# Sums of weight quarters for a seven-part product, made by adding transfers instead of by GpSimd and VectorE

## The chip, the cores and the metric

One Trainium2 chip; the kernel runs on 1 of its cores. The metric is the time of one execution on the device, in microseconds. The core's engines work side by side: TensorE (PE) does matrix products into PSUM, VectorE (DVE), ScalarE (ACT) and GpSimd (POOL) do elementwise work, SyncE (SP) issues most transfers, which 16 DMA engines carry out. GpSimd and ScalarE can issue transfers too. Each engine runs its own queue in order and waits for others by semaphores.

## What is computed

A decoder trunk of four layers on x of 512 tokens by 1024 features in float32. Each layer is a mixer and a dense SwiGLU feed-forward network (FFN), both behind an RMS norm and added to the residual stream:

```python
for i in range(DEPTH):                       # DEPTH = 4
    kind, j = i % 3, i // 3
    h = rmsnorm(x, norm_mix_g[i])
    if kind == 0:   m = short_conv_mixer(h, conv_w_in[j], conv_w[j], conv_w_out[j])
    elif kind == 1: m = chunked_sgu_mixer(h, ...)
    else:           m = retention_mixer(h, ret_w_in[j], ret_w_out[j])
    x = x + m
    h = rmsnorm(x, norm_ffn_g[i])
    x = x + (silu(h @ w_gate[i]) * (h @ w_up[i])) @ w_down[i]   # 1024 -> 2816 -> 1024
return rmsnorm(x, final_norm_g)
```

The products that the change concerns are h @ w_gate, h @ w_up (four FFNs) and h @ conv_w_in (the mixers of layers 0 and 3).

## The kernel before

Features lie on the 128 partitions, tokens along the free dimension. Weights are streamed from HBM in the order of use. The list `chunks` holds that order, and `weights()` prepares up to `AHEAD = 4` chunks ahead, but no further than the first seven-part chunk behind the present one. Every operand is split into two float32r parts, a high one (cast on ScalarE, line 157) and a low one (subtraction on VectorE, line 158), and each product is three matmuls: high by high, high by low, low by high.

The products named above go by Winograd's form of Strassen's method. A chunk is two blocks of 128 output features. Its weights are loaded in two halves of the input features, each half a tile "raw" of 128 x 1024 numbers, 512 KB, which holds four quarters a11, a12, a22 and a21 of 128 KB. `prepare7` makes four sums of quarters in a tile "sums" of the same size: s1, s2 and s4 on GpSimd (lines 131 to 133, each on the result of the one before), s3 on VectorE (line 134). Then three quarters of raw and the four sums are split. `columns7` makes seven products of 12 matmuls of 256 columns each from them, with the right operands xs (quarters of the normed input) and xt (sums of its quarters, from `operand_sums`), and adds up the results in PSUM and with copies in SBUF. The last of the seven parts and what follows (`late`, `held`) are issued while the next chunk is under way. The first chunk of such a layer (in layer 0 the first three) goes by four plain products (`columns4`), which need no sums.

In an FFN the chunks of gate and up alternate; a part of two or three pairs is followed, after the next gate chunk, by `leave`: the down product of the part's hidden features, in 8 blocks of output features of 12 or 18 matmuls of 512 columns.

The pools decide how far loads run ahead: "raw" has 4 buffers, "sums" has 2 (one chunk), the split parts of raw quarters ("w7") and of sums ("wp") have 4 each of high and low. The order of instructions on each engine is set by a scheduler at build time. The rows below write "q" behind an engine for its issuing queue.

Of the kernel before, what the change touches and what calls it, by code (L numbers as in the profile page):

```python
# [17 lines left out]
P = 128  # L18
# [3 lines left out]
NB = D // P            # feature blocks of the residual stream  # L22
NT = T // P            # token blocks
FF = 2816
NF = FF // P
H = T // 2             # tokens of half the sequence
FF_PARTS = ((0, 2), (2, 5), (5, 8), (8, 11))  # pairs of hidden blocks, by part of an FFN
# [8 lines left out]
LAG = 3                # blocks of u that are ahead of the mixing of v  # L36
SOON = 100             # instructions that urgent ones may pass in the scheduler's order
BEGUN = 4              # blocks whose products begin before the last of their operands are ready
AHEAD = 4              # weight chunks prepared ahead of their matmuls


class Kernel:
# [19 lines left out]
    def dense(self):  # L62
        """Memory of the layers whose products take seven parts."""
# [10 lines left out]
    @contextmanager  # L74
    def mixed(self):
        """Memory of the other layers."""
        with self.tc.tile_pool(name="blk", bufs=29, reuse_waits="tile") as self.blk:
            yield

# [17 lines left out]
    def plan7(self, src, plain=False):  # L97
        """Two blocks of columns, for columns4 if plain, else for columns7."""
        self.chunks.append((src, 0, plain))
# [14 lines left out]
    def prepare7(self, i):  # L114
        """Two blocks of columns, as the seven left operands of Winograd's form of Strassen's product."""
# [3 lines left out]
        for half in range(2):  # L119
            raw = self.raw.tile([P, NB // 4, 4, P], F32, tag="raw", name=f"raw{i}{half}")  # L120
            nc.sync.dma_start(raw, src[half])
            if plain:
                h, l = (self.wp.tile([P, NB // 4, 4, P], F32R, tag=part, name=f"w{part}{i}{half}") for part in "hl")
                self.split(raw, h, l)
                for j in range(4):
                    out[j] += [(h[:, k, j], l[:, k, j]) for k in range(NB // 4)]
                continue
            sums = self.sums.tile([P, NB // 4, 4, P], F32, tag="sums", name=f"sums{i}{half}")
            a11, a12, a22, a21 = (raw[:, :, j] for j in range(4))
            s1, s2, s3, s4 = (sums[:, :, j] for j in range(4))  # L130
            nc.gpsimd.tensor_add(s1, a21, a22)  # L131
            nc.gpsimd.tensor_sub(s2, s1, a11)  # L132
            nc.gpsimd.tensor_sub(s4, a12, s2)  # L133
            nc.vector.tensor_sub(s3, a11, a21)  # L134
            for x, n, first, pool in ((raw, 3, 0, self.w7), (sums, 4, 3, self.wp)):
                h, l = (pool.tile([P, NB // 4, n, P], F32R, tag=part, name=f"w{part}{i}{half}{n}") for part in "hl")
                self.split(x[:, :, :n], h, l)
                for j in range(n):
                    out[first + j] += [(h[:, k, j], l[:, k, j]) for k in range(NB // 4)]
# [15 lines left out]
    def split(self, src, h, l):  # L155
        """A float32 tile as two float32r tiles whose sum it is."""
# [9 lines left out]
    def product(self, ps, terms, first=True, last=True, more=False):  # L166
        """ps (+)= sum of lhsT.T @ rhs over (lhs_h, lhs_l, rhs_h, rhs_l), the last term's at the end;
        more: added to a finished sum."""
# [12 lines left out]
    def columns(self, name, acts):  # L181
        """One block of output features (on partitions), for all tokens."""
# [14 lines left out]
    def begin(self, name, acts):  # L197
        """The start of columns(), with the weights of the rest."""
# [5 lines left out]
    def columns7(self, name, then, hold=False):  # L204
        """Two blocks of output features of the residual stream. then() gets them as [P, 2 * T], when the
        next product is under way."""
# [29 lines left out]
        part(c5, 6, xs, 2, False)  # L236
        add(y[:, :H], c5, u2)
        part(c1, 5, xt, 2, False)
        add(y[:, 2 * H : 3 * H], c1, m5)

        def end():
            part(c1, 2, xt, 3, False)
            nc.scalar.copy(y[:, 3 * H :], c1)
# [4 lines left out]
    def columns4(self, name, then, hold=False):  # L248
        """The same by four products of blocks, for which the sums of the operand needn't be ready."""
# [16 lines left out]
    def finish(self, hold=False):  # L266
        """The rest of the last columns7, and what is done with its outcome (and those before it) unless on hold."""
# [8 lines left out]
    def rows(self, name, acts):  # L276
        """512 output features for each block of tokens (on partitions)."""
# [17 lines left out]
    def squares(self, src, add=None):  # L295
        """Running sum, over feature blocks, of the squares."""
# [12 lines left out]
    def rsqrt(self, ps, out, t):  # L309
        """out = ps ** -0.5, with a Newton step."""  # L310
# [7 lines left out]
    def scale_of(self, mean, r, t, *sums):  # L318
        """Each token's 1 / rms, on all partitions."""
# [8 lines left out]
    def diagonal(self, eye):  # L328
        """The matrix that mean_d is the inverse of, on vectors: D on the diagonal."""
# [8 lines left out]
    def scale_of_tokens(self, total):  # L338
        """Each token's 1 / rms, with tokens on partitions: a column for 128 of them."""
# [12 lines left out]
    def spread(self, r, t):  # L352
        """The same on all partitions, in PSUM."""
# [7 lines left out]
    def scale_in_psum(self):  # L361
        """Each token's 1 / rms, on all partitions."""
        return self.spread(self.scale_of_tokens(self.sum), self.hid.tile([P, 2 * T], F32, tag="hid", name="rs")[:, :T])

# [1 line left out]
    def operand(self, m, g):  # L366
        """x's block m as a part of the next product's operand."""
# [592 lines left out]
```

## Time and profile before

| | us |
|---|---|
| median of 2 runs | 2485.22 (2484.79 to 2485.66) |
| span of the profiled execution | 2484.2 |
| TensorE busy in it | 2417.6 (97%) |
| VectorE busy | 1836.7 (74%) |
| ScalarE busy | 1132.3 (46%) |
| GpSimd busy | 890.0 (36%) |

The profile is of one execution, and its span is the time from the first to the last instruction; the median of the runs lies 1.0 us above it. Busy times of engines overlap and don't add up. A group row gives the line of the code, the engine, the operation, the tile written and the tiles read, the shapes and the count, then the busy time in us and the mean of one in ns, and behind the second bar the idle time of the engine just before.

### The profile page before, as it was taken

How to read it: one execution, taken by the hardware profiler on the slowest of the kernel's cores; microseconds unless marked ns; L12 is line 12 of the kernel's file. 1: busy time of each engine (PE TensorE's matmuls, PEld its weight loads, DVE VectorE, ACT ScalarE, POOL GpSimd, SP SyncE). 2: the span in 40 equal slices, each digit the busy share in tenths (PEclk: the TensorE clock that was granted, in tenths of full speed). 3: DMA queues.
4: the chain of work that ended last, by engine and by line, in shares of the span. 5: the costliest groups of instructions: out<-in, count | busy, mean ns of one | idle time of the engine just before them, and what ended most of it. 6: DMA issues, size and time to landing. Idle time of an engine off the chain costs nothing.

```text
span 2484.2 us, 37622 instructions
## 1 busy us (share of the span) xinstructions
PE 2417.6 (97%) x14892; PEld 2179.7 (88%) x14892; DVE 1836.7 (74%) x2236; ACT 1132.3 (46%) x1638; POOL 890.0 (36%) x788
## 2 busy tenths in 40 slices
PE   7999999999999999999999999999999899999998
PEld 6988989988888899998888888799999788889988
DVE  7988878763757887767565465988767898978776
ACT  6455445443324544534333334545435545545443
POOL 5536533520101643442000000834433744733530
PEclk9999999999999999999999999999999999999999
DMA  4141333334332233233223131233234124133231
GB/s 154 62 145 53 116 111 95 97 115 119 94 103 92 68 111 122 88 97 122 95 72 94 60 123 58 91 107 115 85 98 132 52 69 153 52 119 103 85 112 59
DMA packets 78832, 242.09 MB, mean 97 GB/s; under 512 B 8768, under 2 KB 12864, under 8 KB 78656
## 3 DMA queue, kind: packets, MB, share of 16 engines
q1 hardware_dynamic: 77568, 238.65, 30.3%
q8 instruction: 116, 1.90, 0.3%
q10 hardware_dynamic: 1088, 1.05, 0.1%
q14 instruction: 60, 0.49, 0.1%
HBM read 237.56 MB, written 2.10 MB: 96 GB/s over the span
## 4 chain that ended last, share of the span: by engine, by line
PE 75%; DVE 16%; issue 5%; ACT 2%; POOL 1%; DMA 0%; SPq 0%; DVEq 0%; ACTq 0%; POOLq 0%
PE out L177 26%; PE pu L177 16%; PE pg L177 15%; PE pv L177 7%; DVE wl L158 6%; PE pc L177 2%; PE q L177 2%; PE k L177 2%; PE pb L177 2%; DVE sums L134 2%; DVE puy L512 1%; PE pz L177 1%; DVE xl L375 1%; PE po L177 1%; DVE pgy L488 1%
## 5 line engine op out<-in xcount | busy, mean ns | idle before, releaser
L157 ACT CAST wh<-raw 128x768 fp32r<-128x768 f32 (+3 forms) x500 | 425.1, 858 | 572.5 <-PE out L177 193.5
L158 DVE TENSOR_TENSOR wl<-raw,wh 128x768 fp32r<-128x768 f32 (+3 forms) x500 | 557.6, 1134 | 136.7 <-ACT wh L157 136.3
L131 POOL TENSOR_TENSOR sums<-raw 128x256 f32<-128x256 f32 x208 | 243.3, 1170 | 795.8 <-DMA raw<-in_ffn_w_up 360.7
L157 ACT CAST wh<-sums 128x1024 fp32r<-128x1024 f32 x208 | 212.2, 1046 | 182.6 <-POOL sums L133 78.0
L177 PE MATMUL out<-hidl,wh 128*128 128x512 f32 (+1 forms) x736 | 278.3, 380 | 0.0
L158 DVE TENSOR_TENSOR wl<-sums,wh 128x1024 fp32r<-128x1024 f32 x208 | 260.9, 1279 | 22.1 <-ACT wh L157 18.8
L177 PE MATMUL out<-hidh,wh 128*128 128x512 f32 (+1 forms) x736 | 274.6, 381 | 0.0
L133 POOL TENSOR_TENSOR sums<-raw,sums 128x256 f32<-128x256 f32 x208 | 230.1, 1107 | 10.4
L132 POOL TENSOR_TENSOR sums<-sums,raw 128x256 f32<-128x256 f32 x208 | 217.9, 1048 | 10.6
L177 PE MATMUL pg<-xl,wh 128*128 128x256 f32 (+1 forms) x672 | 201.9, 316 | 9.6 <-DVE xl L375 9.6
L422 DVE TENSOR_TENSOR x<-out,x 128x512 f32<-128x512 f32 x192 | 130.2, 683 | 107.0 <-PE out L177 105.9
L177 PE MATMUL out<-hidh,wl 128*128 128x512 f32 (+1 forms) x736 | 205.4, 380 | 0.0
L177 PE MATMUL pg<-xh,wh 128*128 128x256 f32 (+1 forms) x672 | 200.9, 315 | 0.0
L177 PE MATMUL pu<-tl,wh 128*128 128x256 f32 x704 | 185.4, 284 | 5.1 <-DVE tl L158 5.1
L177 PE MATMUL pu<-xl,wh 128*128 128x256 f32 (+1 forms) x656 | 190.0, 306 | 0.0
L177 PE MATMUL pu<-xh,wh 128*128 128x256 f32 (+1 forms) x656 | 189.7, 306 | 0.0
L134 DVE TENSOR_TENSOR sums<-raw 128x256 f32<-128x256 f32 x208 | 153.3, 752 | 44.1 <-DMA raw<-in_ffn_w_up 37.9
L177 PE MATMUL pu<-th,wh 128*128 128x256 f32 x704 | 185.5, 285 | 0.0
L177 PE MATMUL pg<-th,wh 128*128 128x256 f32 x640 | 168.3, 284 | 6.9 <-DVE pgy L224 6.9
L177 PE MATMUL pg<-tl,wh 128*128 128x256 f32 x640 | 167.3, 283 | 0.0
L177 PEld LDWEIGHTS out<-hidl,wh 128*128 128x128 f32 x736 | 138.6, 188 | 25.1
L177 PEld LDWEIGHTS out<-hidh,wh 128*128 128x128 f32 x736 | 137.8, 188 | 25.0
(261 smaller groups left out, 6064.5 us busy)
## 6 DMA issues: line engine op xcount, KB each, us to landing
raw<-in_ffn_w_gate SPq DMA_DIRECT2D x88, 512.0 KB, 3.6
raw<-in_ffn_w_up SPq DMA_DIRECT2D x88, 512.0 KB, 3.6
raw<-in_ffn_w_down SPq DMA_DIRECT2D x96, 384.0 KB, 3.3
raw<-in_conv_w_in SPq DMA_DIRECT2D x48, 512.0 KB, 3.7
raw<-in_sgu_w_v SPq DMA_DIRECT2D x16, 512.0 KB, 3.6
raw<-in_sgu_w_u SPq DMA_DIRECT2D x16, 512.0 KB, 3.5
raw<-in_sgu_w_out SPq DMA_DIRECT2D x16, 512.0 KB, 3.5
raw<-in_ret_w_qk SPq DMA_DIRECT2D x16, 512.0 KB, 3.6
```

The source lines that it names most:

```text
L131: nc.gpsimd.tensor_add(s1, a21, a22)
L132: nc.gpsimd.tensor_sub(s2, s1, a11)
L133: nc.gpsimd.tensor_sub(s4, a12, s2)
L134: nc.vector.tensor_sub(s3, a11, a21)
L157: self.nc.scalar.copy(h, src)
L158: self.nc.vector.tensor_sub(l, src, h.bitcast(F32))
L177: nc.tensor.matmul(ps, x, y, start=first and i == 0, stop=last and i == len(seq) - 1, skip_group_check=more)
L375: nc.vector.scalar_tensor_tensor(l[:, s], x[:, s], gm, h[:, s].bitcast(F32), ALU.mult, ALU.subtract)
L422: nc.vector.tensor_add(x[:, s], ps, x[:, s])
L488: self.nc.vector.tensor_mul(y, y, r.unsqueeze(1).broadcast_to([P, 2, T]))
L512: nc.vector.tensor_mul(y[:, s], y[:, s], g[:, s])
```

## The change

Three of a half's quarters are still loaded into raw (384 KB). The tile of sums is filled by transfers alone: SyncE loads the last quarter into all four places (a load that reads it four times), and three transfers issued by GpSimd add other quarters on top of what lies there: the third quarter to places 1 to 3, the first to places 2 to 4, the second to place 3. Each adds to bytes that the one before has written. The quarters and the sums get another sign and order for this, so that each sum is one of plus signs; the signs are made good where the products are added up (`columns7`: two slots exchanged, one add becomes a multiply by -1 and a subtraction, one copy a multiply by -1) and in the sums of the right operand (`operand_sums`: all four on VectorE, where two had been on GpSimd). The weights are laid out on the host so that a quarter is 1 KB in a row on each partition. Comments and docstrings went too.

```diff
 def prepare7(self, i):
-            raw = self.raw.tile([P, NB // 4, 4, P], F32, tag="raw", name=f"raw{i}{half}")
-            nc.sync.dma_start(raw, src[half])
...
-            sums = self.sums.tile([P, NB // 4, 4, P], F32, tag="sums", name=f"sums{i}{half}")
-            a11, a12, a22, a21 = (raw[:, :, j] for j in range(4))
-            s1, s2, s3, s4 = (sums[:, :, j] for j in range(4))
-            nc.gpsimd.tensor_add(s1, a21, a22)
-            nc.gpsimd.tensor_sub(s2, s1, a11)
-            nc.gpsimd.tensor_sub(s4, a12, s2)
-            nc.vector.tensor_sub(s3, a11, a21)
+            raw = self.raw.tile([P, 3, NB // 4, P], F32, tag="raw", name=f"raw{i}{half}")
+            sums = self.sums.tile([P, 4, NB // 4, P], F32, tag="sums", name=f"sums{i}{half}")
+            block = lambda j, n=1: src[half][:, j : j + 1].broadcast_to([P, n, NB // 4, P])
+            nc.sync.dma_start(raw, src[half][:, :3])
+            nc.sync.dma_start(sums, block(3, 4))
+            nc.gpsimd.dma_start(sums[:, :3], block(2, 3), accum_op=ALU.add)
+            nc.gpsimd.dma_start(sums[:, 1:], block(0, 3), accum_op=ALU.add)
+            nc.gpsimd.dma_start(sums[:, 2:3], block(1), accum_op=ALU.add)
             for x, n, first, pool in ((raw, 3, 0, self.w7), (sums, 4, 3, self.wp)):
-                self.split(x[:, :, :n], h, l)
+                self.split(x, h, l)
 def columns7(self, name, then, hold=False):
-        part(c5, 6, xs, 2, False)
+        part(c5, 5, xs, 2, False)
         add(y[:, :H], c5, u2)
-        part(c1, 5, xt, 2, False)
-        add(y[:, 2 * H : 3 * H], c1, m5)
+        part(c1, 6, xt, 2, False)
+        with self.tc.high_priority(SOON):
+            nc.vector.scalar_tensor_tensor(y[:, 2 * H : 3 * H], c1, -1.0, m5, ALU.mult, ALU.subtract)
...
-            nc.scalar.copy(y[:, 3 * H :], c1)
+            nc.scalar.mul(y[:, 3 * H :], c1, -1.0)
 def operand_sums(self, k, g):
-        nc.vector.tensor_sub(t1, b12, b11)
-        nc.gpsimd.tensor_sub(t2, b22, t1)
+        nc.vector.tensor_sub(t1, b11, b12)
         nc.vector.tensor_sub(t3, b22, b12)
-        nc.gpsimd.tensor_sub(t4, b21, t2)
+        nc.vector.scalar_tensor_tensor(t2, t1, -1.0, b22, ALU.mult, ALU.subtract)
+        nc.vector.scalar_tensor_tensor(t4, t2, -1.0, b21, ALU.mult, ALU.subtract)
```

How it moves instructions, at one place in the first FFN, where the chunk of an up product follows that of a gate product. On GpSimd before, the sums of the two halves of a gate chunk (its tiles are sums_3094 and sums_3109 before, sums_3093 and sums_3108 now; the number behind a tile is its place in the program; a row names line, operation, tile written, tiles read, shape and the semaphores waited for):

```order
L131 TENSOR_TENSOR sums_3094<-raw_3092 128x2x128 [waits DMAHW6_49,DVE_49]
L132 TENSOR_TENSOR sums_3094<-sums_3094,raw_3092 128x2x128 [waits Pool_49]
L131 TENSOR_TENSOR sums_3109<-raw_3107 128x2x128 [waits DMAHW7_49,DVE_49]
L133 TENSOR_TENSOR sums_3094<-raw_3092,sums_3094 128x2x128 [waits Pool_49]
L132 TENSOR_TENSOR sums_3109<-sums_3109,raw_3107 128x2x128 [waits Pool_49]
L133 TENSOR_TENSOR sums_3109<-raw_3107,sums_3109 128x2x128 [waits Pool_49]
```

GpSimd now, for the same chunk and for the one before it; "DMAHW" is the landing of a load by SyncE, "DMASW" that of a transfer issued by GpSimd:

```order
L134 DMA sums_2960<-in_ffn_w_up 128x3x256 [waits DMAHW6_49,DMASW0_49,DVE_49]
L134 DMA sums_2975<-in_ffn_w_up 128x3x256 [waits DMAHW7_49,DMASW1_49,DVE_49]
L135 DMA sums_2960<-in_ffn_w_up 128x3x256 [waits DMASW2_49]
L135 DMA sums_2975<-in_ffn_w_up 128x3x256 [waits DMASW3_49]
L136 DMA sums_2960<-in_ffn_w_up 128x256 [waits DMASW4_49]
L136 DMA sums_2975<-in_ffn_w_up 128x256 [waits DMASW5_49]
L134 DMA sums_3093<-in_ffn_w_gate 128x3x256 [waits DMAHW2_49,DMASW6_49,DVE_49]
L134 DMA sums_3108<-in_ffn_w_gate 128x3x256 [waits DMAHW3_49,DMASW7_49,DVE_49]
L135 DMA sums_3093<-in_ffn_w_gate 128x3x256 [waits DMASW0_49]
L135 DMA sums_3108<-in_ffn_w_gate 128x3x256 [waits DMASW1_49]
L136 DMA sums_3093<-in_ffn_w_gate 128x256 [waits DMASW2_49]
L136 DMA sums_3108<-in_ffn_w_gate 128x256 [waits DMASW3_49]
```

Three operations on data for each half have become three transfers for each half, taken in turn for the two halves; each waits for the landing of the one before it on the same half, and the first also for the load by SyncE and for VectorE's last use of the buffer.

On SyncE before, the loads of three chunks (two halves each) around the same place:

```order
L121 DMA raw_2959<-in_ffn_w_up 128x1024 [waits DMAHW0_49,DVE_49,Pool_49]
L121 DMA raw_2974<-in_ffn_w_up 128x1024 [waits DMAHW1_49,DVE_49,Pool_49]
L121 DMA raw_3092<-in_ffn_w_gate 128x1024 [waits DMAHW2_49,DVE_49,Pool_49]
L121 DMA raw_3107<-in_ffn_w_gate 128x1024 [waits DMAHW3_49,DVE_49,Pool_49]
L121 DMA raw_3223<-in_ffn_w_up 128x1024 [waits DMAHW4_49,DVE_49,Pool_49]
L121 DMA raw_3238<-in_ffn_w_up 128x1024 [waits DMAHW5_49,DVE_49,Pool_49]
```

SyncE now:

```order
L132 DMA raw_2959<-in_ffn_w_up 128x768 [waits DMAHW4_49,DVE_49]
L132 DMA raw_2974<-in_ffn_w_up 128x768 [waits DMAHW5_49,DVE_49]
L132 DMA raw_3092<-in_ffn_w_gate 128x768 [waits DMAHW6_49,DVE_49]
L132 DMA raw_3107<-in_ffn_w_gate 128x768 [waits DMAHW0_49,DVE_49]
L133 DMA sums_2960<-in_ffn_w_up 128x4x256 [waits DMASW6_49,DMASW4_49,DMAHW7_49,DMASW0_49,DVE_49]
L133 DMA sums_2975<-in_ffn_w_up 128x4x256 [waits DMASW7_49,DMASW5_49,DMAHW1_49,DMASW1_49,DVE_49]
L132 DMA raw_3223<-in_ffn_w_up 128x768 [waits DMAHW2_49,DVE_49]
L132 DMA raw_3238<-in_ffn_w_up 128x768 [waits DMAHW3_49,DVE_49]
L133 DMA sums_3093<-in_ffn_w_gate 128x4x256 [waits DMASW6_49,DMASW4_49,DMAHW6_49,DMASW2_49,DVE_49]
L133 DMA sums_3108<-in_ffn_w_gate 128x4x256 [waits DMASW7_49,DMASW5_49,DMAHW7_49,DMASW3_49,DVE_49]
```

Each half has two loads in place of one. The load into the sums of a chunk (sums_3093) stands behind the raw loads of the chunk after it (raw_3223), and waits for VectorE's subtraction from the same buffer's former sums.

On ScalarE now, the casts of the sums of the same chunk and what stands around them:

```order
L229 COPY pgm<-pg_3253 128x256 [waits PE_49]
L159 CAST wh_3230<-raw_3223 128x768 [waits DMAHW0_49,PE_49]
L159 CAST wh_3245<-raw_3238 128x768 [waits DMAHW1_49,PE_49]
L246 ACTIVATE puy<-pu_3122 128x256 [waits PE_49]
L159 CAST hidh<-puy 128x1024 [waits DVE_49]
L159 CAST wh_3103<-sums_3093 128x1024 [waits DMASW4_49,DMAHW2_49,DMASW2_49,DMASW0_49]
L159 CAST wh_3118<-sums_3108 128x1024 [waits DMASW5_49,DMAHW3_49,DMASW3_49,DMASW1_49]
L231 COPY pgm<-pg_3254 128x256 [waits PE_49]
L235 COPY pgm<-pg_3253 128x256 [waits PE_49]
```

The same place of ScalarE before:

```order
L157 CAST wh_2981<-raw_2974 128x768 [waits DMAHW5_49,PE_49]
L243 COPY puy<-pu_2874 128x256 [waits PE_49]
L157 CAST hidh<-puy 128x1024 [waits DVE_49]
L157 CAST wh_3103<-sums_3094 128x1024 [waits PE_49,Pool_49]
L157 CAST wh_3118<-sums_3109 128x1024 [waits PE_49,Pool_49]
L227 COPY pum<-pu_3122 128x256 [waits PE_49]
L229 COPY pum<-pu_3123 128x256 [waits DVE_49,PE_49]
L157 CAST wh_3099<-raw_3092 128x768 [waits DMAHW6_49,PE_49]
L157 CAST wh_3114<-raw_3107 128x768 [waits DMAHW7_49,PE_49]
L243 COPY pgy<-pg_2989 128x256 [waits PE_49]
```

The casts stand where they stood, behind the end of the chunk before and ahead of the copies of the next part's results (pgm, line 231 now); what they wait for is no longer GpSimd but the landings of four transfers.

## Rows read from the trace of the kernel before

**Rows 1.** The page: span, and busy time of each engine.
```profile
span 2484.2 us, 37622 instructions
...
PE 2417.6 (97%) x14892; PEld 2179.7 (88%) x14892; DVE 1836.7 (74%) x2236; ACT 1132.3 (46%) x1638; POOL 890.0 (36%) x788
```

**Rows 2.** The chain that ended last: start us, us, what; one part, and a down product.
```profile
286.13 2.88 PE pg L177 x24
289.01 1.45 PE pu L177 x12
...
344.38 25.87 PE out L177 x114
```

**Rows 3.** Timeline of SyncE's queue, dense stretch: start us, us, engine, line, operation, count.
```profile
292.10 1.74 SPq L121 DMA_DIRECT2D raw<-in_ffn_w_up  x2
302.98 1.74 SPq L121 DMA_DIRECT2D raw<-in_ffn_w_gate  x2
313.64 19.78 SPq L108 DMA_DIRECT2D raw<-in_ffn_w_down  x8
```

**Rows 4.** Busy time by window, two chunks of the dense stretch; columns in the first row.
```profile
core 0: us, PE busy (x) PEld busy (x) DVE busy (x) ACT busy (x) POOL busy (x), PEclk, DMA share, GB/s
292.10:313.64 21.54, 21.54 (x182) 21.54 (x181) 20.96 (x23) 11.39 (x18) 14.67 (x13) 1.00 0.31 99
```

**Rows 5.** Waits (us in total, times, longest), and GpSimd's timeline for one chunk.
```profile
POOL sums L131 <- DVE wl L158: 355.3, 107, 11.0
...
298.69 1.65 POOL L131 TENSOR_TENSOR sums<-raw 128x256 f32<-128x256 f32 x1 [2.95 <-DVE wl L158]
300.42 0.80 POOL L132 TENSOR_TENSOR sums<-sums,raw 128x256 f32<-128x256 f32 x1
...
305.00 0.74 POOL L133 TENSOR_TENSOR sums<-raw,sums 128x256 f32<-128x256 f32 x1
```

**Rows 6.** Instructions on tile "sums", 290 to 330 us: ns min/median/max, first and last start.
```profile
L157 ACT CAST wh<-sums x6: 1028/1044/1050, 296.1 to 318.6; 128x1024 fp32r<-128x1024 f32 x6
L158 DVE TENSOR_TENSOR wl<-sums,wh x6: 1214/1218/1220, 297.4 to 320.4; 128x1024 fp32r<-128x1024 f32 x6
```

**Rows 7.** Groups of instructions: what | busy us, mean ns | idle before, releaser.
```profile
L131 POOL TENSOR_TENSOR sums<-raw 128x256 f32<-128x256 f32 x208 | 243.3, 1170 | 795.8 <-DMA raw<-in_ffn_w_up 360.7
...
L132 POOL TENSOR_TENSOR sums<-sums,raw 128x256 f32<-128x256 f32 x208 | 217.9, 1048 | 10.6
...
L133 POOL TENSOR_TENSOR sums<-raw,sums 128x256 f32<-128x256 f32 x208 | 230.1, 1107 | 10.4
...
L134 DVE TENSOR_TENSOR sums<-raw 128x256 f32<-128x256 f32 x208 | 153.3, 752 | 44.1 <-DMA raw<-in_ffn_w_up 37.9
```

**Rows 8.** VectorE's timeline, dense stretch: sums by VectorE, and adds from PSUM.
```profile
299.66 1.84 DVE L134 TENSOR_TENSOR sums<-raw 128x256 f32<-128x256 f32 x2
...
307.72 0.42 DVE L224 TENSOR_TENSOR puy<-pu,pum 128x256 f32<-128x256 f32 x1
```

**Rows 9.** DMA: queue (packets, MB, share of engines); issues with KB each, us to landing.
```profile
q1 hardware_dynamic: 77568, 238.65, 30.3%
...
raw<-in_ffn_w_gate SPq DMA_DIRECT2D x88, 512.0 KB, 3.6
...
raw<-in_ffn_w_down SPq DMA_DIRECT2D x96, 384.0 KB, 3.3
...
raw<-in_conv_w_out SPq DMA_DIRECT2D x16, 128.0 KB, 2.1
```

More of the change, by code (lines that the diff above doesn't have):

```diff
@@ L119, in prepare7 @@
         for half in range(2):
-            raw = self.raw.tile([P, NB // 4, 4, P], F32, tag="raw", name=f"raw{i}{half}")
-            nc.sync.dma_start(raw, src[half])
             if plain:
-                h, l = (self.wp.tile([P, NB // 4, 4, P], F32R, tag=part, name=f"w{part}{i}{half}") for part in "hl")
+                raw = self.raw.tile([P, 4, NB // 4, P], F32, tag="raw", name=f"raw{i}{half}")
+                nc.sync.dma_start(raw, src[half])
+                h, l = (self.wp.tile([P, 4, NB // 4, P], F32R, tag=part, name=f"w{part}{i}{half}") for part in "hl")
@@ L124, in prepare7 @@
                 self.split(raw, h, l)
                 for j in range(4):
-                    out[j] += [(h[:, k, j], l[:, k, j]) for k in range(NB // 4)]
+                    out[j] += [(h[:, j, k], l[:, j, k]) for k in range(NB // 4)]
                 continue
-            sums = self.sums.tile([P, NB // 4, 4, P], F32, tag="sums", name=f"sums{i}{half}")
-            a11, a12, a22, a21 = (raw[:, :, j] for j in range(4))
-            s1, s2, s3, s4 = (sums[:, :, j] for j in range(4))
-            nc.gpsimd.tensor_add(s1, a21, a22)
@@ L135, in prepare7 @@
+            nc.gpsimd.dma_start(sums[:, :3], block(2, 3), accum_op=ALU.add)
+            nc.gpsimd.dma_start(sums[:, 1:], block(0, 3), accum_op=ALU.add)
+            nc.gpsimd.dma_start(sums[:, 2:3], block(1), accum_op=ALU.add)
             for x, n, first, pool in ((raw, 3, 0, self.w7), (sums, 4, 3, self.wp)):
-                h, l = (pool.tile([P, NB // 4, n, P], F32R, tag=part, name=f"w{part}{i}{half}{n}") for part in "hl")
-                self.split(x[:, :, :n], h, l)
+                h, l = (pool.tile([P, n, NB // 4, P], F32R, tag=part, name=f"w{part}{i}{half}{n}") for part in "hl")
+                self.split(x, h, l)
@@ L138, in prepare7 @@
                 for j in range(n):
-                    out[first + j] += [(h[:, k, j], l[:, k, j]) for k in range(NB // 4)]
+                    out[first + j] += [(h[:, j, k], l[:, j, k]) for k in range(NB // 4)]
         return out
@@ L880, in columns_by_two @@
     n, k, m = w.shape
-    w = w.reshape(n, 2, k // (4 * P), 2, P, m // (2 * P), 2, P).transpose(0, 5, 1, 4, 2, 6, 3, 7)
-    return np.ascontiguousarray(w.reshape(n, m // (2 * P), 2, P, k // (4 * P), 4, P)[..., [0, 1, 3, 2], :])
+    w = w.reshape(n, 2, k // (4 * P), 2, P, m // (2 * P), 2, P).transpose(0, 5, 1, 4, 6, 3, 2, 7)
+    return np.ascontiguousarray(w.reshape(n, m // (2 * P), 2, P, 4, k // (4 * P), P)[:, :, :, :, [0, 1, 3, 2]])
 def columns_first(w, parts=1):
```

## The prediction

> **What bounds the kernel now.** I read the busy shares first, then one dense stretch, then who releases the buffers of the sums. TensorE is busy for 2417.6 of 2484.2 us [rows 1], so all its idle time is 67 us, and no change to the other engines can give more than that: 2.7% of the span. TensorE's own need for one two-block chunk of a seven-part product is small and exact. A part is 12 matmuls and takes 1.44 to 1.45 us [rows 2], so seven parts take 7 x 1.44 = 10.1 us. Yet in a stretch of nothing but such chunks the loads of two chunks follow each other every 302.98 - 292.10 = 10.9 us and 313.64 - 302.98 = 10.7 us [rows 3]. The gap between 10.1 and 10.7 is VectorE's: over 292.10 to 313.64 it is busy for 20.96 of 21.54 us, at a granted TensorE clock of 1.00 [rows 4]. So in dense stretches VectorE sets the pace by a little and TensorE comes right behind it; elsewhere TensorE sets it. Period now: 10.7 us.
>
> The last thing to see is how a sum is made. There are only two buffers for sums, one for each half of a chunk. GpSimd begins a new chunk's sums when VectorE has finished the low part of the old ones: that wait is put down to "wl" of line 158, 107 times [rows 5]. From there GpSimd needs 298.69 to 305.74, 7.05 us for both halves [rows 5]. Then ScalarE casts (1.04 us) and VectorE subtracts (1.22 us) each half [rows 6], and the buffers are free again. The loop from buffer free to buffer free thus has to fit into 10.7 us, and does, because the raw weights had been loaded long before.
>
> **What the change removes.** On GpSimd: 208 of each of lines 131, 132 and 133, 243.3 + 217.9 + 230.1 = 691 us [rows 7]. GpSimd is busy 36% [rows 1], so this alone is worth nothing. On VectorE: 208 of line 134, 153.3 us [rows 7], or in the dense stretch two at 0.92 us for each chunk (1.84 us at 299.66 [rows 8]). That would bring VectorE from 10.5 to 8.6 us for each chunk, under TensorE's 10.1, and would give back 0.6 us a chunk. VectorE takes over two of four subtractions of each operand's sums from GpSimd, 48 in all. The nearest row of that size with operands in SBUF is line 134, 0.75 us: 48 x 0.75 = 36 us [rows 7], between 24 places of layer ends; against 153 us taken away it counts for nothing. Negating copies in place of copies, and scalar_tensor_tensor in place of an add of the same 128x256 from PSUM (0.42 us [rows 8]), I cost at nothing: same engine, same size.
>
> **What the change adds: bytes.** A quarter of half a chunk is 128 KB. Before, a half loaded four. After, it loads 3 (raw) + 4 (the last quarter, four times over) and adds 3 + 3 + 1: 14 quarters, 1.75 MB, so 3.67 MB for a chunk. The queue moved 238.65 MB in 30.3% of 16 engines' span [rows 9]: 238.65 / (0.303 x 2484.2) = 317 GB/s when it runs. At that rate 3.67 MB take 11.6 us, already more than TensorE's 10.1. An addition must fetch the old value too; if each added byte counts twice, 14 additions of quarters become 28 and the chunk takes 17.4 us of all 16 engines.
>
> **What the change adds: a chain.** This is the term that decides. The buffer of sums now passes through four transfers in a row, each waiting for the one before to land, and then through the cast and the subtraction, before the next load into it may start. The order of GpSimd's queue is load A, load B, then first addition A, B, second A, B, third A, B; the halves overlap, the four steps of one half do not. No adding transfer and none issued by GpSimd stands in the trace, so I bound them. Lower bound, from landings of plain loads alone on the queue: 512 KB in 3.6 us, 384 KB in 3.3 us, 128 KB in 2.1 us [rows 9]. So 3.6 + 3.3 + 3.3 + 2.1 = 12.3 us, plus 1.04 + 1.22 for the split = 14.6 us for one buffer's loop. Upper bound: the same landings are about 1.6 us fixed plus 0.5 us for each 128 KB. Let the added bytes count twice, and let the other half, which is always one step behind, double each transfer's moving part: load 1.6 + 4.0, first and second addition 1.6 + 6.0 each, third 1.6 + 2.0, split 2.3: 26.7 us. The middle is 20.7, and the engines' 17.4 us of work leave little room below; I take a period of 21 us. A gain on this path is excluded: even the lower bound is above 10.7.
>
> The Trainium skill (DMA: Bandwidth & Descriptors, "Anatomy of one DMA") fits a transfer issued by GpSimd as 2.0 us plus bytes over 436 GB/s; as an estimate by that the four steps take 3.2 + 2.9 + 2.9 + 2.3 = 11.3 us, the loop 13.6 us and the kernel some 2690 us. No run before shows such a transfer, but the plain landings [rows 9] are longer at every size. The skill's Collectives: The Full Stack ("The bandwidth ceiling") says that an adding step reads two sources and so runs at half the rate of a copy; that is what speaks most against this change, and by it the upper bound is the nearer one.
>
> **How often it is paid.** There are 104 such chunks (208 halves [rows 7]). Lookahead does not help, since two buffers hold just one chunk: while TensorE works on chunk i, only chunk i+1 can be under way. In an FFN, 21 seven-part chunks follow each other with three stretches of the down product between; 17 of the 20 intervals are bare. The 8 output blocks of such a stretch take 114 matmuls in 25.87 us [rows 2], 0.227 us each, so 96 or 144 of them take 22 or 33 us: with the chunk's own 10 us that hides a whole chain, and most of the next one's. I count 14 bare intervals for an FFN, 56 for four, and 7 and 9 in the two convolutions (9 and 11 chunks, one short down stretch each): 72. Each goes from 10.7 to 21: 72 x 10.3 = 742 us. The sum goes on the profiled execution's 2484.2 us, which is 1 us under the median of 2485.22: 3226, say **3230 us**.
>
> What queues behind the new wait: on ScalarE the copies of the next part's accumulator stand behind the waiting cast, so TensorE stops within one or two parts; on GpSimd the second and third additions of both halves wait in order behind the first; on SyncE the raw loads of the chunk after next stand behind the load into the sums. None of these lengthens the loop, since they wait for the same thing.
>
> **Rivals.** (a) The chain is the bound, between 15 and 29.7 us: 72 x 4.3 to 72 x 19 = 310 to 1370 us more, 2800 to 3850. Chance 0.80. (b) Adding transfers are far dearer than a doubled load, say twice the upper half of my bound, 32 us: 72 x 21.3 = 1530, some 4020 us. For it: pieces of 1 KB in place of 4 KB, descriptors written by software; against it: no row. 0.12. (c) The halves interleave so well that only bytes bind, 11.6 us: 72 x 0.9 = 65 us, 2550 us. Against it: the single landings above. 0.05. (d) Not slower: the transfers keep up with TensorE, VectorE and GpSimd are relieved, and TensorE's idle time goes, at best 2484 - 67 = 2417 us. It needs the four steps in 10.7 - 2.3 = 8.4 us, 2.1 us each, the landing of 128 KB, where three of them carry 384 or 512 KB. 0.03.
>
> The range of 2800 to 3850 leaves (b), (c) and (d) out, 0.20 together. About 2% is what a measurement of this kernel can tell from no change. Faster by more needs 50 of the 67 us: 0.01. Within 2%: the rest of (d) and part of (c), 0.04. Slower: 0.95.
>
> **What would show it.** In the profile after: GpSimd's and VectorE's rows of lines 131 to 134 gone; bytes up by 208 x 1.25 MB = 273 MB to some 515 MB; loads into "sums" in dense stretches 15 to 28 us apart in place of 10.7; TensorE idle there for about half the time, waiting in turn for the cast or the subtraction of the sums, which wait for a GpSimd DMA; the down stretches and the SGU and retention layers unchanged in length. I would be wrong if adding transfers land in about 2 us each whatever their size, if the scheduler's order lets TensorE run over the waits for more than one chunk, or, on the other side, if GpSimd takes several us to issue each transfer.

## The result, and the profile after

| | before | after |
|---|---|---|
| median of 2 runs, us | 2485.22 | 3523.01 (3518.91 to 3527.10) |
| ratio | 1 | 1.4174 (95% interval 1.4147 to 1.4201) |
| span of the profiled execution, us | 2484.2 | 3517.2 |

The kernel became 42% slower. The forecast was 3230 us, in a range of 2800 to 3850, with the loop of the sums' buffers as the likeliest cause.

The page of the kernel after, the lines that answer to [rows 1] and [rows 9]: span, busy times, then the queues with packets, MB and their share of 16 engines, then issues with KB each and median us to landing, and last the chain's shares by engine.

```profile
span 3517.2 us, 38464 instructions
...
PE 2640.1 (75%) x14892; PEld 2368.1 (67%) x14892; DVE 1613.2 (46%) x2076; ACT 1134.1 (32%) x1638; POOL 864.7 (25%) x740
...
DMA packets 385015, 514.83 MB, mean 146 GB/s; under 512 B 22080, under 2 KB 319040, under 8 KB 384832
...
q0 software_dynamic: 196352, 190.88, 35.6%
q1 hardware_dynamic: 187392, 320.45, 29.3%
...
DMA 52%; PE 27%; issue 9%; DVE 6%; ACT 3%; POOL 2%; ACTq 0%; POOLq 0%; DVEq 0%; SPq 0%
...
sums<-in_ffn_w_up POOLq DMA_DIRECT2D x176, 384.0 KB, 6.1
sums<-in_ffn_w_gate POOLq DMA_DIRECT2D x160, 384.0 KB, 5.5
sums<-in_ffn_w_up SPq DMA_DIRECT2D x88, 512.0 KB, 4.4
...
sums<-in_ffn_w_up POOLq DMA_DIRECT2D x88, 128.0 KB, 3.1
```

None of the five engines is near its limit any more, and over half of the chain that ended last is transfers. VectorE has less to do than before. GpSimd's busy time hardly fell (890.0 to 864.7 us), because issuing the 624 adding transfers is work of its own: without them, in run 4 below, it is busy for 160.3 us. SyncE's loads into the sums in a dense stretch, beside [rows 3] (start us, us, engine, line, operation, count):

```profile
398.74 2.42 SPq L133 DMA_DIRECT2D sums<-in_ffn_w_up  x2
...
422.53 2.37 SPq L133 DMA_DIRECT2D sums<-in_ffn_w_gate  x2
...
448.02 2.98 SPq L133 DMA_DIRECT2D sums<-in_ffn_w_up  x2
```

Chunks now follow each other every 23.8 and 25.5 us in place of 10.7; the median of the 80 such intervals inside the four FFNs is 24.9. What fills one of them stands in the chain (start us, us, what):

```profile
422.19 1.05 ACT wh L159
...
423.26 1.24 DVE wl L160
424.51 5.73 DMA sums<-in_ffn_w_gate
...
430.31 0.51 issue
430.82 5.30 DMA sums<-in_ffn_w_gate
436.12 0.29 issue
436.41 8.45 DMA sums<-in_ffn_w_gate
444.86 0.28 issue
445.15 2.99 DMA sums<-in_ffn_w_gate
...
448.29 1.05 ACT wh L159
```

From cast to cast, 448.29 - 422.19 = 26.1 us, the buffer of one half of a chunk goes through cast, subtraction, load and three additions, one behind the other, with nothing of TensorE in between. The same stretch by windows, two of 25 us and three that follow the additions of this chain (columns in the first row):

```profile
core 0: us, PE busy (x) PEld busy (x) DVE busy (x) ACT busy (x) POOL busy (x), PEclk, DMA share, GB/s
400.00:425.00 25.00, 17.77 (x121) 17.56 (x122) 9.75 (x13) 7.90 (x13) 6.87 (x6) 0.77 0.77 161
425.00:450.00 25.00, 12.67 (x84) 12.26 (x83) 10.71 (x13) 7.05 (x10) 6.87 (x6) 0.70 0.79 173
...
430.80:436.10 5.30, 3.65 (x29) 3.25 (x27) 2.68 (x5) 1.95 (x3) 2.55 (x2) 1.00 0.95 160
436.40:444.90 8.50, 0.00 (x0) 0.00 (x0) 2.70 (x3) 1.04 (x1) 2.18 (x2) 0.56 0.98 200
445.10:448.20 3.10, 1.41 (x6) 1.42 (x7) 1.23 (x1) 1.04 (x1) 0.86 (x1) 0.50 0.28 43
```

Over 25 us the DMA engines are busy for 0.77 to 0.79, so bytes alone don't explain the period. But within the loop they are not evenly busy: during the first and second additions they are full (0.95 and 0.98), during the last one nearly idle (0.28), and the window of the second addition holds no matmul at all. Last, the waits (us in total, times, longest):

```profile
ACT wh L159 <- DMA sums<-in_ffn_w_gate: 508.4, 73, 18.4
ACT wh L159 <- DMA sums<-in_ffn_w_up: 387.3, 64, 12.3
...
PE pg L179 <- ACT wh L159: 256.5, 34, 13.5
...
PE pu L179 <- ACT wh L159: 201.6, 24, 13.7
...
PE pu L179 <- ACT pum L229: 128.1, 11, 21.6
...
PE pg L179 <- ACT pgm L231: 66.8, 7, 12.7
```

ScalarE's cast waits for the transfers, and TensorE for the cast, or for a copy of its own earlier results (pum, pgm) that stands behind the cast in ScalarE's queue.

### The profile page after: what moved, and what is told of

It reads as the page before. It is cut to its first block, busy times and chain, and to the rows that moved or that the text cites. A ratio compares the mean times of both kernels' runs of the same rounds, so it can differ in the third digit from the quotient of the medians.

```text
span 3517.2 us, 38464 instructions
## 1 busy us (share of the span) xinstructions
PE 2640.1 (75%) x14892; PEld 2368.1 (67%) x14892; DVE 1613.2 (46%) x2076; ACT 1134.1 (32%) x1638; POOL 864.7 (25%) x740
## 2 busy tenths in 40 slices
DMA packets 385015, 514.83 MB, mean 146 GB/s; under 512 B 22080, under 2 KB 319040, under 8 KB 384832
## 3 DMA queue, kind: packets, MB, share of 16 engines
q0 software_dynamic: 196352, 190.88, 35.6%
q1 hardware_dynamic: 187392, 320.45, 29.3%
## 4 chain that ended last, share of the span: by engine, by line
DMA 52%; PE 27%; issue 9%; DVE 6%; ACT 3%; POOL 2%; ACTq 0%; POOLq 0%; DVEq 0%; SPq 0%
DMA sums<-in_ffn_w_up 21%; DMA sums<-in_ffn_w_gate 20%; DMA sums<-in_conv_w_in 10%; PE out L179 8%; PE pv L179 5%; PE pu L179 4%; PE pg L179 4%; DVE wl L160 3%; ACT wh L159 3%; PE q L179 1%; PE k L179 1%; POOL sums L135 1%; PE po L179 1%; PE pb L179 1%; DVE x L425 1%
## 5 line engine op out<-in xcount | busy, mean ns | idle before, releaser
L160 DVE TENSOR_TENSOR wl<-raw,wh 128x768 fp32r<-128x768 f32 (+3 forms) x500 | 487.4, 993 | 220.6 <-ACT wh L159 215.9
L159 ACT CAST wh<-sums 128x1024 fp32r<-128x1024 f32 x208 | 217.2, 1045 | 1126.6 <-DMA sums<-in_ffn_w_gate 508.4
L179 PE MATMUL pu<-th,wh 128*128 128x256 f32 x704 | 216.3, 322 | 338.9 <-ACT wh L159 195.8
L179 PEld LDWEIGHTS pu<-th,wh 128*128 128x128 f32 x704 | 154.7, 220 | 351.4 <-ACT wh L159 200.5
L179 PE MATMUL pg<-th,wh 128*128 128x256 f32 x640 | 198.4, 324 | 247.6 <-ACT wh L159 230.2
L179 PEld LDWEIGHTS pg<-th,wh 128*128 128x128 f32 x640 | 142.3, 222 | 258.3 <-ACT wh L159 236.7
L179 PE MATMUL pg<-xh,wh 128*128 128x256 f32 (+1 forms) x672 | 226.4, 348 | 94.2 <-ACT pgm L231 66.8
L179 PEld LDWEIGHTS pg<-xh,wh 128*128 128x128 f32 x672 | 148.7, 222 | 105.3 <-ACT pgm L231 69.0
L134 POOL DMA_DIRECT2D sums<-in_ffn_w_up x88 | 115.0, 1309 | 331.5 <-DMA sums<-in_ffn_w_up 207.0
L134 POOL DMA_DIRECT2D sums<-in_ffn_w_gate x80 | 106.9, 1337 | 330.5 <-DMA sums<-in_ffn_w_gate 162.0
L179 PE MATMUL pg<-xh,wl 128*128 128x256 f32 (+1 forms) x672 | 163.8, 338 | 0.0
```

The costliest lines, as they stand in the source:

```text
L134: nc.gpsimd.dma_start(sums[:, :3], block(2, 3), accum_op=ALU.add)
L159: self.nc.scalar.copy(h, src)
L160: self.nc.vector.tensor_sub(l, src, h.bitcast(F32))
L179: nc.tensor.matmul(ps, x, y, start=first and i == 0, stop=last and i == len(seq) - 1, skip_group_check=more)
```

## The experiments

Two theories were to be told apart. **Chain**: the loop of one buffer through four dependent transfers is the period, and only two buffers exist. **Bytes**: adding transfers occupy the 16 engines for so long that their sum is the period. A third question was what the sums of before cost at all, which is the most that any such change can give. Times with a ratio and its interval are medians of several executions; the others are of one execution, beside a kernel before of 2485.6 to 2486.5 us. Where a kernel ran more than once here, its times lie within 0.3% of each other, so differences under 1% are not read from them.

**1. Parts of the change that have nothing to do with transfers.** The signs that make each sum one of plus signs, and the new layout, with sums still made by the engines (from a raw tile of four quarters, whose lines are left out here):

```diff
...
+            nc.gpsimd.tensor_add(s0, b3, b2)
+            nc.gpsimd.tensor_add(s1, s0, b0)
+            nc.gpsimd.tensor_add(s2, s1, b1)
+            nc.vector.tensor_add(s3, b3, b0)
```

> The new signs, the new order of quarters in memory and the two subtractions moved to VectorE alone; the sums are made as before, s0 = b3 + b2, s1 = s0 + b0, s2 = s1 + b1 by GpSimd and s3 = b3 + b0 by VectorE, from a raw tile of four quarters. Theory of the chain (the four transfers in a row through two buffers are the whole loss): within 0.5% of before, 2475 to 2497 us. Rival, that signs, layout or the moved subtractions carry part of the loss: over 2510 us.

Measured: 2487.92 us, ratio 1.0005 (0.9995 to 1.0014). The signs, the layout and VectorE's 48 extra subtractions cost nothing that shows; the whole loss is the transfers'.

**2. One sum less on VectorE.** From run 1, the last sum on GpSimd instead:

```diff
-            nc.vector.tensor_add(s3, b3, b0)
+            nc.gpsimd.tensor_add(s3, b3, b0)
```

> No transfers add; the fourth sum moves from VectorE to GpSimd. GpSimd's sums for a chunk go from 7.05 us to some 9 us, under TensorE's 10.1; VectorE is relieved of 1.84 us. If VectorE's load is what held dense stretches at 10.7 us: 2430 to 2475 us. If GpSimd's longer chain then ends last: 2490 to 2560 us.

Measured: 2487.43 us, ratio 1.0003 (0.9994 to 1.0013). Neither side came true. The page of this run, and a wait of ScalarE:

```profile
PE 2422.7 (97%) x14892; PEld 2183.5 (88%) x14892; DVE 1742.7 (70%) x2076; ACT 1134.3 (46%) x1638; POOL 1025.2 (41%) x948
...
ACT wh L160 <- POOL sums L136: 189.9, 110, 5.9
```

VectorE is relieved of 1836.7 - 1742.7 = 94 us [rows 1] and nothing is gained. By itself this does not show that VectorE cost nothing, for the other side's cause is at work too: ScalarE's casts wait for GpSimd's sums of line 136 for 189.9 us, where it was 63.1 in run 1. TensorE's waits for VectorE stay almost as they were, 39 us in all against 40 in run 1.

**3. One sum by one transfer.** From run 1, the last sum loaded and added:

```diff
-            nc.vector.tensor_add(s3, b3, b0)
+            nc.sync.dma_start(s3, src[half][:, 3])
+            nc.gpsimd.dma_start(s3, src[half][:, 0], accum_op=ALU.add)
```

> Only the fourth sum is made by transfers: a load of 128 KB into its place and one adding transfer of 128 KB; the other three by GpSimd from a raw tile of four quarters. Theory of the chain: the loop of this buffer is a 128 KB load (some 2.5 us), one addition (3.1 us after) and the split (2.3 us), some 8 us, and fits into TensorE's 10.1; VectorE is rid of 153 us, so dense stretches go from 10.7 to near 10.1 us for each chunk: 2420 to 2470 us. Rival, that any adding transfer on GpSimd's queue holds up the sums behind it: over 2500 us.

Measured: 2549.51 us, ratio 1.0253 (1.0238 to 1.0268): the rival. VectorE had 64 us less to do [rows 1] and yet the kernel lost 2.5%. Its landings (KB, median us) and waits:

```profile
sums<-in_ffn_w_up POOLq DMA_DIRECT2D x88, 128.0 KB, 3.7
```

```profile
ACT wh L161 <- DMA sums<-in_ffn_w_gate: 67.4, 28, 6.9
...
ACT wh L161 <- DMA sums<-in_ffn_w_up: 54.9, 25, 4.1
ACT wh L161 <- DMA sums<-in_conv_w_in: 47.5, 17, 7.5
```

A single 128 KB addition, 3.7 us and behind a load, is already late for the cast in 70 of 208 halves: the two cannot begin before the buffer is free. The rival's own cause shows as well: GpSimd's queue stands at the adding transfer for 57.5 + 28.3 + 11.4 us, waiting for the load to land, with its sums behind it. Which of the two weighs more was not tried apart. Of the 62 us over run 1, 24 are longer busy time of TensorE (2443.0 in place of 2418.8 us, at a granted clock of 0.985 in place of 0.993).

**4. A ladder: how many additions in the chain.** From the kernel after, the third addition's line left out, then the second's too, then all three:

```diff
             nc.sync.dma_start(sums, block(3, 4))
             nc.gpsimd.dma_start(sums[:, :3], block(2, 3), accum_op=ALU.add)
-            nc.gpsimd.dma_start(sums[:, 1:], block(0, 3), accum_op=ALU.add)
-            nc.gpsimd.dma_start(sums[:, 2:3], block(1), accum_op=ALU.add)
```

> The third adding transfer (128 KB onto one place) is left out, so that one sum lacks a term. Theory of the chain: its landing of 3.0 us and the issue around it, 3.5 us together, go from each of 104 loops: 3517 - 364 = about 3150 us. Rival, that the bytes of the 16 engines set the pace: 2 of 42 quarters of work go, 5% of 18 us or 0.9 us a chunk: about 3425 us.

> The changed kernel with the first adding transfer alone, 384 KB (two additions are left out). Theory of the chain: the loop is 4.5 + 5.5 for the transfers, 2.3 for the split and 0.8 of issue, 13.1 us against TensorE's 10.1; the down products take some of it back, so 72 x 3.0 = 216 us more: 2620 to 2740 us. If bytes set the pace (20 quarters of work a chunk, 8.3 us): about 2490 us.

> The changed kernel without its three adding transfers: the last quarter is still loaded four times into the sums (the additions are left out). Theory of the chain: the loop is 4.4 us of load, 2.3 of split and 0.5 of issue, 7.2 us, under TensorE's 10.1: 2470 to 2510 us. Rival, that the doubled loads and bytes already cost: over 2540 us.

| additions in the chain | time, us | more than the step above | period inside the FFNs (median), us |
|---|---|---|---|
| 0 | 2432.30 | | |
| 1 (384 KB) | 2687.06 | 255 | 15.3 |
| 2 (384 + 384 KB) | 3169.08 | 482 | 21.5 |
| 3 (384 + 384 + 128 KB) | 3523.01 | 354 | 24.9 |

The third addition moves 1/7 of the added bytes and costs 354 of 1091 us: it is paid as a link of a chain, as expected. By bytes alone its step would have been 156 us. With no addition the kernel comes out under what was expected, and as fast as one without sums (run 5): the load that reads one quarter four times over costs nothing by itself, although it raises the loaded bytes from 238.65 to 320.45 MB.

**5. No sums at all.** The raw quarters are used in place of the sums:

```diff
-            for x, n, first, pool in ((raw, 3, 0, self.w7), (sums, 4, 3, self.wp)):
+            for x, n, first, pool in ((raw, 3, 0, self.w7), (raw, 4, 3, self.wp)):
```

> The changed kernel with no sums made at all: raw quarters are split and multiplied in their place (part of the computation is left out). It is the most that any way of making the sums could give back. If VectorE's and GpSimd's work on the sums held the kernel before: 2415 to 2450 us. If that work was hidden behind TensorE (as the run with the fourth sum on GpSimd, 94 us less of VectorE and no gain, would have it): 2470 to 2490 us.

Measured: 2431.06 us, in the range of the first expectation. Its page:

```profile
PE 2401.4 (99%) x14892; PEld 2169.6 (89%) x14892; DVE 1604.7 (66%) x2076; ACT 1143.5 (47%) x1638; POOL 155.6 (6%) x116
```

All making of sums in the kernel before is worth 2486.5 - 2431.1 = 55 us, 2.2%. TensorE is then at 99%. In the profiled executions, TensorE's idle time goes from 67 to 28 us and its busy time from 2417.6 to 2401.4. Its waits for VectorE add up to 46 us before and to 11 here, so VectorE, which makes one of the sums and is slower while GpSimd makes the others (last section), did hold TensorE up a little. By this run, no way of making the sums wins much more.

**6. Copies in place of additions.** Same transfers, same bytes, same order, without `accum_op` in all three lines:

```diff
-            nc.gpsimd.dma_start(sums[:, :3], block(2, 3), accum_op=ALU.add)
+            nc.gpsimd.dma_start(sums[:, :3], block(2, 3))
...
```

> The three transfers issued by GpSimd copy instead of adding: same pieces, same bytes, same order and waits, but no old value is read (the sums are left out by this). Theory that adding doubles a transfer's work: the loop goes from some 24.5 us to 4.4 + 4.5 + 5.0 + 2.5 for the transfers and 3.4 for split and issue, 19.8: about 3030 us. Rival, that the price is GpSimd's issuing and its descriptors, adding or not: unchanged, about 3500 us. Rival, that only the engines' bytes count: 28 quarters of work instead of 42, 12 us a chunk: about 2600 us.

Measured: 3171.47 us, between the expectations and 351.5 us below the kernel after. The queue of GpSimd's transfers, a landing, and a window of 25 us, to be held against the rows above; last, the load queue of the kernel without additions (run 4):

```profile
q0 software_dynamic: 56576, 190.88, 18.4%
...
sums<-in_ffn_w_up POOLq DMA_DIRECT2D x176, 384.0 KB, 4.3
...
400.00:425.00 25.00, 15.92 (x105) 15.52 (x105) 8.40 (x11) 7.15 (x10) 4.17 (x6) 0.77 0.53 171
```

```profile
q1 hardware_dynamic: 187392, 320.45, 41.4%
```

As copies, 190.88 MB take 0.184 x 3169.7 = 583 us of all engines, 327 GB/s; as additions 0.356 x 3517.2 = 1252 us, 152 GB/s, in 3.5 times as many packets. Adding costs the engines 2.1 times as much as copying. Smaller pieces alone are not the reason: in the trace of the kernel after, a packet of 1 KB keeps an engine busy for 106 ns on the mean as an addition and for 55 ns as a load by SyncE. And without additions the load queue, with such packets among its own, moves 320.45 / (0.414 x 2430.2) = 319 GB/s, where it was 317 before the change. But a chain of copies is still 686 us slower than before, with the DMA engines busy for only 0.53 of the window: most of the loss needs no adding.

**7. Half the bytes in the additions**, in as many pieces (`sums[:, :3, :1]` and so on).

> The three adding transfers carry half the bytes, one of two row blocks of each quarter (the other half of the additions is left out); same number of pieces, half as long, same order and waits. If an adding transfer's time goes with its bytes: the loop goes from 24.5 to about 19.3 us, about 2980 us. If it goes with the number of pieces: at most 1 us less in the loop, about 3400 us. If only the engines' bytes set the pace: about 2600 us.

Measured: 3286.49 us, between both. Its queue:

```profile
q0 software_dynamic: 196352, 95.46, 23.8%
```

With half the bytes the engines still need 0.238 x 3284.7 = 782 of 1252 us. If the time is a part for the pieces and a part for the bytes, the bytes' is 2 x 470 = 940 us and the pieces' 312: about 3 to 1.

**8. One more buffer for sums.** Two tile pools changed: sums from 2 to 3, and raw from 4 to 3 to make room; the control has only the second.

```diff
-        self.raw = pool("raw", 4)
+        self.raw = pool("raw", 3)
...
-            self.tc.tile_pool(name="sums", bufs=2, reuse_waits="tile") as self.sums,
+            self.tc.tile_pool(name="sums", bufs=3, reuse_waits="tile") as self.sums,
```

> Control for the next run: the changed kernel with 3 buffers of raw weights instead of 4. Under every theory the raw weights are early while the sums are late: 3490 to 3580 us.

> The changed kernel with 3 buffers of sums instead of 2 (and 3 of raw, so that they fit): three half chunks may be under way. Theory of the chain: the loop of a buffer stays or grows with sharing, but one and a half chunks share it, so the period falls toward the engines' own 18 us, as far as GpSimd's order lets it: 2900 to 3250 us. Rival, that the bytes of the 16 engines set the pace: as the control, no change.

Measured: control 3468.59, third buffer 3178.65 us, a gain of 290 us with the same transfers, bytes and additions. So the reuse of the buffers does hold the loop back. Two windows of the run with three:

```profile
380.00:420.00 40.00, 28.73 (x209) 28.32 (x209) 19.06 (x23) 13.90 (x23) 12.65 (x11) 0.87 0.94 200
...
2000.00:2060.00 60.00, 51.44 (x312) 47.00 (x312) 30.00 (x40) 19.72 (x32) 18.59 (x16) 0.91 0.94 205
```

The DMA share is now 0.94, where it was 0.77: with that wait eased, the engines' own time is close to being the next bound. That the control is 1.5% faster than the kernel after was not expected and stays unexplained.

**9. Both together:** copies, and three buffers for sums.

> Both at once: plain copies in place of the adding transfers (the sums are left out by this) and 3 buffers of sums with 3 of raw. If the loop and the doubled work of an addition are the whole loss, what is left is the bytes of 28 quarters, 3.67 MB at 311 GB/s = 11.8 us a chunk, where TensorE needs 10.1: 2600 to 2750 us. If GpSimd's in-order queue holds one half behind the other: 2850 us or more.

Measured: 2788.99 us, 39 above the range of the one and under the bound of the other expectation. Relief adds up: copies give 351.5 us with two buffers and 390 with three, a third buffer gives 290 with additions. What is left, 357 us over a kernel without additions, is not full engines, as two windows of this run show:

```profile
380.00:420.00 40.00, 39.86 (x211) 34.24 (x210) 24.54 (x30) 16.26 (x23) 8.59 (x13) 1.00 0.76 244
420.00:460.00 40.00, 30.25 (x237) 29.64 (x236) 14.35 (x19) 11.82 (x20) 8.92 (x14) 0.96 0.64 205
```

At 0.64 to 0.76 the loop itself is likely still too long; the order of GpSimd's queue, which three buffers must share, was not tried apart.

No version that makes all the sums beat the kernel before. The most that could be won is 55 us, and the mildest use of an adding transfer (run 3) lost 63.

## Why the prediction held, and where it was off

**The ceiling (67 us, nothing else to win): right.** Taking all sums away gives 55 us (run 5): 39 of TensorE's idle time, and 16 of its busy time, which the ceiling had not counted.

**VectorE sets the pace of 10.7 us in dense stretches: wrong.** [Rows 4] themselves say so: TensorE was busy for 21.54 of 21.54 us. Its 182 matmuls there are all of gate and up, one every 1.44 / 12 = 0.12 us, and are a little more than two chunks (168): the distance between two loads is not the pace of the chunks, which is TensorE's own. Run 2 agrees: 94 us off VectorE, no gain. VectorE does hold TensorE up a little elsewhere, by the waits told in run 5. The error cost the forecast nothing, since the change lengthens the period whichever of the two had set it, but it would have misjudged a change that relieves VectorE alone: the expectations of runs 2 and 3 were built on it and both fell.

**Work removed, worth little: right by the margin of the ceiling, but mis-sized.** VectorE's busy time fell by 223 us where 117 were forecast (last section), and GpSimd got the issuing in place of its sums. With the additions left out, the removal shows as 54 us (run 4).

**Bytes: right.** 514.83 MB against some 515. That added bytes count twice was put as a condition; run 6 shows 152 against 327 GB/s. In the sum for one chunk: 1252 / 104 = 12.0 us for additions and 1.84 MB (14 quarters) at 320.45 / (0.293 x 3517.2) = 311 GB/s, 5.9 us, for its loads, 17.9 together where 17.4 was forecast. The Trainium skill (Collectives: The Full Stack, "The bandwidth ceiling") gives half the rate for the adding step of a collective, because it reads two sources, and the trace agrees in the rate. The other rule of the Trainium skill that stood in the prediction, 2.0 us plus bytes over 436 GB/s for a transfer issued by GpSimd (DMA: Bandwidth & Descriptors, "Anatomy of one DMA"), makes 384 KB 2.9 us, as an estimate; here, beside other transfers, a copy took 4.3 and an addition 5.5 to 6.1 us, so the measurement decides.

**The chain is the bound: right in mechanism, mis-sized.** The failed term is the period of 21 us, taken as the middle between 14.6 and 26.7. It was 24.9. Of the terms, in the loop shown above: load 5.73 (3.6 to 5.6), first addition 5.30 and second 8.45 (3.3 to 7.6 each), third 2.99 (2.1 to 3.6), split 2.3 (2.3). Two things were missing. The second addition runs beside the other half's second and third (434.45 to 445.54 us) and two loads of down weights of 384 KB (435.90 to 442.90), and the windows show the engines full for its 8.5 us: here the doubled bytes and the chain meet, and the upper bound, not the middle, is what holds. And between landing and next transfer lie 0.5, 0.3 and 0.3 us of issue on GpSimd, which the sum left out. A forecast from the upper bound would have read the rows better: the prediction said that 17.4 us of engines' work leaves little room below 21, but a chain that leaves the engines at 0.28 in one of its steps needs more room than that.

**72 bare intervals: in agreement, not proved.** 72 x (24.9 - 10.7) = 1022 us, and the spans differ by 1033; from TensorE's own 10.1 it would be 1066. For shorter chains the same count comes out too high: two additions 72 x (21.5 - 10.7) = 778, where the spans differ by 683; one addition 72 x (15.3 - 10.7) = 331, measured 201. Where the chain is shorter more intervals are covered by the down products, so the close match for the kernel after is partly luck. The 80 intervals counted run from 21 to 44 us, so the loop has no single period either.

**What queues behind: right.** ScalarE's cast waits for 508.4 + 387.3 us on the FFNs' sums, and TensorE waits both for it and for the copies behind it (pum, pgm).

**The rivals.** (b), far dearer additions: did not come, for the period stayed under the 26.7 of (a); the bytes' rate was halved, which (a) had allowed for, and GpSimd needs 0.9 to 1.3 us to issue one, not several. (c), bytes alone: refuted by the DMA share of 0.77 and by the third buffer, though run 8 shows that it comes close behind. (d), the transfers keep up: refuted already by the single addition of run 3.

A clock that no step had: the matmuls' busy time rose from 2417.6 to 2640.1 us for the same 14892 matmuls, 222 us, at a granted clock of 0.87 over the span. In the kernel after it likely lies beside the loop of the sums, which goes on while TensorE computes; that was not tried apart. With one addition it stands in the chain; the three rows below are TensorE's timeline after a wait (in brackets: the wait and what ended it), the chain, and the window:

```profile
458.47 0.58 PE L177 MATMUL pu<-th,wh 128*128 128x256 f32 x1 [3.68 <-ACT pum L227]
```

```profile
458.47 5.49 PE pu L177 x24
463.96 1.52 PE pg L177 x12
```

```profile
458.47:463.96 5.49, 5.49 (x25) 5.49 (x26) 5.11 (x6) 3.27 (x6) 0.00 (x0) 0.50 0.48 128
```

After 3.68 us without work the granted clock is 0.50, 1.2 GHz: 24 matmuls take 5.49 us, 0.229 each, and the next 12 take 1.52, 0.127 each. This wait thus costs 3.68 us and, by the rows at both levels, 24 x (0.229 - 0.120) = 2.6 us more.

## What to carry to other kernels

When work moves from an engine into a row of dependent transfers, time the loop from buffer free to buffer free against the period it has to fit into, with the transfers at the rate they have when all of them run at once; the loop of four was 24.9 us against 10.7, and engines that were relieved gave nothing back. Look first at the idle time of the engine that is nearly full: it tells about how much any relief of the others can be worth (67 us of idle time here, 55 us won when all sums were gone), before anything is spent on it.

## What was not expected of the hardware

**VectorE is slower while GpSimd computes.** Two groups of VectorE's instructions (line, operation, tiles, shapes, count | busy us, mean ns), before and after; last the first group in run 1, with the new layout and GpSimd's sums:

```profile
L158 DVE TENSOR_TENSOR wl<-raw,wh 128x768 fp32r<-128x768 f32 x320 | 365.3, 1168 | 29.6 <-ACT wh L157 29.6
...
L224 DVE TENSOR_TENSOR puy<-pu,pum 128x256 f32<-128x256 f32 x132 | 53.5, 418 | 90.6 <-PE pu L177 90.0
```

```profile
L160 DVE TENSOR_TENSOR wl<-raw,wh 128x768 fp32r<-128x768 f32 x320 | 299.5, 962 | 115.8 <-ACT wh L159 113.7 <-PE pz L179 1.7
...
L226 DVE TENSOR_TENSOR puy<-pu,pum 128x256 f32<-128x256 f32 x88 | 37.1, 422 | 134.7 <-PE pu L179 134.4
```

```profile
L161 DVE TENSOR_TENSOR wl<-raw,wh 128x768 fp32r<-128x768 f32 x320 | 361.3, 1155 | 34.1 <-ACT wh L160 34.1
```

A subtraction with both operands in SBUF went from 1168 to 962 ns when GpSimd stopped adding, while an addition with an operand in PSUM stayed at 418 to 422. The layout is not the cause: with it and GpSimd's sums the mean is 1155. Nor does GpSimd's issuing of transfers have this effect: 962 ns in the kernel after, where GpSimd is busy for 864.7 us, mostly with that, and 963 in run 5, where it is busy for 155.6. VectorE's busy time fell by 223 us and not by the 117 forecast, and 66 us of it are this one group; in run 2, where GpSimd makes all sums, it has 138 us more to do than in run 5 with the same 2076 instructions. The Trainium skill (GPSIMD Engine Reference, "8. Key points") says that GpSimd shares its SBUF interfaces with VectorE and contends with instructions that have two SBUF inputs; the trace agrees.

**An addition is split finer than a copy.** The same 190.88 MB went in 196352 packets as additions and 56576 as copies, and, if their time is a part for the pieces and a part for the bytes, about a quarter of it goes with the number of pieces (run 7).

**A load that reads its source four times lands somewhat later than a plain one of its size, and cost this kernel nothing by itself:** 512 KB in 4.4 us here, and in 4.3 to 4.5 without additions, beside 3.6 us for a plain load [rows 9]; without additions the kernel with it is as fast as one that makes no sums (2432.30 and 2431.06 us).
